# Cumulated decays from a scratch in HBM instead of through TensorE, a pause between a planner's steps, and a copy moved to ScalarE

## The chip, the cores and the metric

One core of a Trainium2 chip runs the whole program. Its engines are TensorE (PE, matrix products and transposes into PSUM), VectorE (DVE), ScalarE (ACT), GpSimd (POOL) and SyncE (SP, which here only issues transfers). Each works its own queue in order and waits for others by semaphores. The metric is the device time of one execution in microseconds (us), as the median of several runs. The profile is one further execution, taken by the hardware profiler.

## The reference

Two layers over 256 tokens of width 1024, and a final norm. The first layer is a mixture of a state space part (SSD, 16 heads of 64) and a gated linear attention (GLA, 8 heads); the second is a causal attention of 16 heads of 64, with a gate. The part that the change touches is the SSD's decay and the GLA's inner product:

```python
def ssd_chunked_scan(xs, dt, a, bm, cm, d_skip):
    ...
    a_cs = jnp.cumsum(dt_c * a, axis=2)
    a_t = jnp.moveaxis(a_cs, 2, -1)
    seg = a_t[..., :, None] - a_t[..., None, :]
    causal = jnp.tril(jnp.ones((Q, Q), dtype=bool))
    decay_ij = jnp.exp(jnp.where(causal, seg, -jnp.inf))
    cb = jnp.einsum('bcign,bcjgn->bcgij', c_c, b_c)
    y_diag = jnp.einsum('bcgeij,bcjgep->bcigep', cb[:, :, :, None] * decay_ij, xdt)
    ...

def ssd_gla_layer(x, ...):
    h = rms_norm(x, norm_w)
    u = h @ w_in
    ...
    y_a = ssd_chunked_scan(xs, dt, a, bm, cm, d)
    y_a = rms_norm(y_a * jax.nn.silu(z_a), ssd_norm_w)
    ...
    o_b = gla_chunked(q_b, k_b, v_b, log_decay)
    o_b = rms_norm(o_b, gla_norm_w) * jax.nn.silu(g_b)
    out = jnp.concatenate([y_a, o_b], axis=-1) @ w_out
    return x + out
```

The kernel must give `rms_norm(x, final_norm)` of both layers' result.

## The kernel before

**Products and weights.** Every large product runs in three parts: weights and activations are cut into a high and a low part (`h_`, `l_`), and high by high, high by low and low by high are summed in PSUM (`mm3`). Weights arrive in pieces of 512 KB or less through SP's queue (`fetch`) into four raw buffers; ScalarE copies the high part (L77) and VectorE subtracts for the low one (L78) into one of seven buffers (`NW`). `need` cuts pieces up to three ahead of the one in use (`AHEAD` = 4). Stages follow one another on TensorE: `pa` and `pb` (input projections of layer 1; `pa` with 416 columns, `pb` with 256), `pc` (output projection, columns from GLA `c1`, from SSD `c0`), `pv` (values of layer 2, two halves `n` of 512 columns, in each two tiles `tt` of 128 tokens, 8 blocks `kb` of three products), `pp` (queries, keys, gates of layer 2) and `pf` (output projection).

**Planner.** All small work beside these products is written as generators (`co_...`) that yield a delay. A clock (`clock["now"]`) advances by an estimated time with each product (`spend`); after each block of three products `due()` runs every generator whose time has come. So the code is written in one fixed order at build time: on TensorE, VectorE and ScalarE the order of instructions follows from it. The delays stand in the table `DL`.

**The mixer** (some 40 to 165 us). `co_first` computes the time steps `dt`, their cumulated decay `acp` (16 heads by 256 tokens), its copy `acT`, a high-low cut of it `ahl`, and by transposes the form with tokens on partitions, `acs`. `co_pair` handles two blocks of two heads: a transpose of `xs` (`xtp`) gives `xdt` (VectorE, L509); for each head a product of a column of ones (`sel`) with `ahl` (`ab`, a small PSUM tile) brings that head's decays to all 128 partitions; ScalarE forms relu(acs - ab) into `e` (L516, L518) and its exponential (L520), VectorE multiplies by the scores `cbT` (L521). After a delay the group `yp` multiplies `e` by `xdt`, and VectorE adds the skip into `y` (L533). `co_gla_pair` handles two heads: scores `gs`; ScalarE copies them to `sT` (L604), POOL masks them (L605), VectorE adds one crossing block (L607); then the values' products `go`, the norm of each head (ScalarE squares, VectorE, POOL's power L625, VectorE), the gated result `ob` (L629), and its transposes `obt` (L163), cut into `obhi` and `oblo`.

**Small PSUM tiles.** `pm` gives one of four small PSUM tiles. A request waits until the last reader of the tile's previous holder is done.

**Between the layers.** `co_turn` transposes a part of `x1` (`htp`, four blocks of 128 columns): for each block ScalarE writes the high part (L741), VectorE the low part (L742), into the activations that `pv` reads (`h`). `co_norm` and its `rb1p` bring the norm's factors to all partitions.

Of the kernel before, what the change touches and what calls it, by code (L numbers as in the profile page):

```python
# [37 lines left out]
C_DTB, C_AL = 79, 95  # L38
C_N = 111

M_ID, M_TRI, M_MASK, M_SEL = 0, 128, 384, 768
M_N = 784


@with_exitstack
def trunk(ctx, tc, xw_d, x_d, cst_d, mat_d, gw2_d, fn_d, wa_d, wb_d, wc_d, wv_d, wp_d, wf_d, out_d):
# [79 lines left out]

    clock = {"now": 0.0, "seq": 0}
    waiting = []  # L130

    def spend(ns):
# [75 lines left out]
    tri = [mat[:, M_TRI + P * i:M_TRI + P * i + P] for i in range(2)]  # L208
    mask = mat[:, M_MASK:M_MASK + 3 * P]
    ones = cpool.tile([P, 1], F32, name="ones")  # L210
    mhalf = cpool.tile([P, 2], F32, name="mhalf")
    V.memset(ones, 1.0)
    V.memset(mhalf, -0.5)
    scanm = big.tile([P, 16, 64], F32, name="scanm", tag="s3")
# [149 lines left out]
    acT = cpool.tile([16, T], F32, name="acT")
    ahl = cpool.tile([P, T], F32R, name="ahl")
    sel = cpool.tile([P, 16], F32R, name="sel")
    G.memset(ahl.bitcast(F32), 0.0)


    gl3 = cpool.tile([P, T], F32R, name="gl3")  # L370
# [7 lines left out]
    def co_first(ps):  # L378
# [38 lines left out]
        for tt in range(2):  # L417
            mm(acp[0:16, tt * P:tt * P + P], dta[:, tt, :], tri[tt])
        V.tensor_copy(acT, acp[0:16, 0:T])
        S.activation(ahl[0:16, :], acp[0:16, 0:T], AF.Copy)  # L420
        V.tensor_sub(ahl[32:48, :], acT, ahl[0:16, :].bitcast(F32))
        V.tensor_copy(sel, mat[:, M_SEL:M_SEL + 16])
        yield DL["act"]
        act = pm("act")
        for tt in range(2):
# [72 lines left out]
    def co_pair(*blks):  # L498


        rows = [slice(64 * j, 64 * j + 64) for j in range(2)]
        es, xds = [], []
        for i, blk in enumerate(blks):
            yield DL[f"pair{i}"]
            tp = pm(f"xtp{blk}")
            for tt in range(2):
                tr(tp[:, tt * P:tt * P + P], xs[:, blk, tt * P:tt * P + P])
            xdt = tmp.tile([P, 2, 2, 64], F32, name=f"xdt{blk}", tag="t1c", bufs=3)
            V.tensor_tensor(xdt, tp[:, 0:T].rearrange("p (a b c) -> p a b c", a=2, b=2),  # L509
                            dt[:, :, 2 * blk:2 * blk + 2][:, :, :, None].to_broadcast([P, 2, 2, 64]), op=ALU.mult)  # L510
            e = tmp.tile([P, 2, 3, P], F32, name=f"e{blk}", tag="t3", bufs=3)
            for j in range(2):
                h = 2 * blk + j
                ab = pm(f"ab{h}")
                mm(ab[:, 0:T], sel[:, h:h + 1].to_broadcast([P, P]), ahl)
                S.activation(e[:, j, 0:2, :].rearrange("p a b -> p (a b)"), ab[:, 0:T], AF.Relu, scale=-1.0,  # L516
                             bias=acs[:, 0, h:h + 1])
                S.activation(e[:, j, 2, :], ab[:, P:T], AF.Relu, scale=-1.0, bias=acs[:, 1, h:h + 1])  # L518
            ef = e.rearrange("p a b c -> p (a b c)")
            S.activation(ef, ef, AF.Exp, scale=-1.0)  # L520
            V.tensor_tensor(e, e, cbT[blk // 4].rearrange("p (a b) -> p a b", a=3)[:, None, :, :]  # L521
                            .to_broadcast([P, 2, 3, P]), op=ALU.mult)
            es.append(e)
# [60 lines left out]
    def co_gla_pair(b):  # L584
# [17 lines left out]
        for h, sp_ in zip(heads, sps):  # L602
            sT = tmp.tile([P, 3, P], F32, name=f"sT{h}", tag="t1d")
            S.activation(sT.rearrange("p a b -> p (a b)"), sp_[:, 0:3 * P], AF.Copy)  # L604
            G.affine_select(out=sT[:, 0:3:2, :], in_=sT[:, 0:3:2, :], pattern=[[0, 2], [1, P]],  # L605
                            compare_op=ALU.is_ge, fill=0.0, base=0, channel_multiplier=-1)
            V.tensor_copy(sT[0:64, 0:3:2, 64:P], sp_[0:64, 384:512].rearrange("p (a b) -> p a b", a=2))  # L607
            sTs.append(sT)
        yield DL["gla1"]
        obs = []  # L610
        for h, sT in zip(heads, sTs):
# [6 lines left out]
            ss = sm.tile([P, 2], F32, name=f"oss{h}", tag="oss")  # L618
            for tt in range(2):
                S.activation(sq[:, tt * P:tt * P + P], op[:, tt * P:tt * P + P], AF.Square,  # L620
                             accum_out=ss[:, tt:tt + 1])
            rr = sm.tile([P, 2], F32, name=f"rr{h}", tag="rr")
            V.tensor_tensor(ss, ss, rsv, op=ALU.mult)
            V.tensor_scalar(ss, ss, EPS, None, op0=ALU.add)
            G.tensor_tensor(rr, ss, mhalf, op=ALU.pow)  # L625
            V.tensor_tensor(rr, rr, rsh, op=ALU.mult)
            ob = tmp.tile([P, T], F32, name=f"ob{h}", tag="t1f")
            for tt in range(2):
                V.scalar_tensor_tensor(ob[:, tt * P:tt * P + P], op[:, tt * P:tt * P + P], rr[:, tt:tt + 1],  # L629
                                       gs[:, tt, vc], op0=ALU.mult, op1=ALU.mult)  # L630
            obs.append(ob)
        yield DL["gla2"]
# [116 lines left out]
    def co_norm():  # L749
        s = sm.tile([P, 2], F32, name="sn", tag="sn")  # L750
        V.tensor_tensor(s, ssn[:, :, 0], ssn[:, :, 1], op=ALU.add)
        V.tensor_scalar(s, s, 1.0 / D, EPS, op0=ALU.mult, op1=ALU.add)
        G.tensor_tensor(r1, s, mhalf, op=ALU.pow)
        V.tensor_scalar(rq, r1, -0.125, None, op0=ALU.mult)
        env["r1"] = True
        yield DL["rb1"]
# [185 lines left out]
def _pack(inp):  # L942
# [73 lines left out]
```

## Time and profile before

| | us |
|---|---|
| median of 3 runs | 340.42 |
| lowest, highest | 338.98, 341.65 |
| profiled execution | 340.22 |
| its span | 338.5 |
| TensorE busy in the span | 327.8 (97%) |
| VectorE, ScalarE, GpSimd busy | 259.4, 232.7, 27.1 |

The span is the time from the first to the last instruction of the profiled execution; 1.7 us of the execution lie around it. Busy time of TensorE counts pipelined products by modelled ends, so that a busy engine need not be at its peak rate: how long a product costs is read from the distance of its start to that of the next one, not from its length. In the rows below, an idle time before an instruction stands in brackets with what ended it.

### The profile page before, as it was taken

Reading aid. Unit: us, or ns where it says so; the run is one execution under the profiler, and the core shown is the slowest. Engines: PE = TensorE matmul, PEld = TensorE weight load, DVE = VectorE, ACT = ScalarE, POOL = GpSimd, SP = SyncE. Lnnn points to the kernel's source line nnn. Section 1 sums busy time; section 2 is a strip of 40 time slices with the busy share of each in tenths; the row PEclk is TensorE's granted clock in tenths of the full one; section 3 lists DMA queues with packets and bytes.
Section 4 is the critical chain, followed back from the end, with each engine's and each line's share of the span. In section 5 each row is a group of like instructions: output and inputs, shape, how many; then the busy total and the mean of one; then the engine's idle time right before and its main releaser. Section 6 shows DMA issues by size and latency. Waiting matters only on the chain.

```text
span 338.5 us, 5905 instructions
## 1 busy us (share of the span) xinstructions
PE 327.8 (97%) x2153; PEld 293.9 (87%) x2153; DVE 259.4 (77%) x543; ACT 232.7 (69%) x501; POOL 27.1 (8%) x44
## 2 busy tenths in 40 slices
PE   8999999999997999999999999999999999999992
PEld 8999999999996979999888888888888887888792
DVE  4978978999999587689964775467869699696563
ACT  6858789959868646678352676475696996969420
POOL 2010000000001211344200000000000000000010
PEclk9999999999999999999999999999999999999997
DMA  7985582575427346241685635756408146070003
GB/s 294 406 266 180 166 257 103 178 241 190 135 95 255 124 141 216 80 152 36 221 286 179 192 122 184 248 166 222 173 24 287 65 141 232 1 248 3 0 2 125
DMA packets 16254, 56.15 MB, mean 166 GB/s; under 512 B 1968, under 2 KB 2480, under 8 KB 16096
## 3 DMA queue, kind: packets, MB, share of 16 engines
q1 hardware_dynamic: 15360, 53.37, 46.6%
q10 hardware_dynamic: 864, 2.39, 2.0%
q8 instruction: 17, 0.28, 0.3%
q14 instruction: 13, 0.11, 0.1%
HBM read 54.71 MB, written 1.05 MB: 165 GB/s over the span
## 4 chain that ended last, share of the span: by engine, by line
PE 49%; DVE 20%; ACT 17%; issue 6%; DMA 4%; POOL 2%; POOLq 0%; ACTq 0%; DVEq 0%
PE pc L159 13%; PE pp L159 10%; PE pv L159 6%; PE pa L159 6%; PE pf L159 5%; DVE l_b L78 3%; PE pb L159 3%; DMA r_b<-in_wb 3%; ACT h_p L77 3%; DVE cu L467 2%; DVE l_p L78 2%; ACT pt L810 2%; ACT h_b L77 2%; ACT pt L814 2%; POOL rr L625 1%
## 5 line engine op out<-in xcount | busy, mean ns | idle before, releaser
L159 PE MATMUL pb<-hh,h_b 128*128 128x256 f32 x416 | 76.4, 285 | 0.0
L159 PE MATMUL pp<-h,h_p 128*128 128x512 f32 x192 | 67.3, 402 | 0.0
L159 PEld LDWEIGHTS pb<-hh,h_b 128*128 128x128 f32 x416 | 64.8, 191 | 0.4 <-issue 0.2
L159 PE MATMUL pb<-hh,l_b 128*128 128x256 f32 x208 | 58.8, 283 | 0.0
L159 PE MATMUL pp<-h,l_p 128*128 128x256 f32 x192 | 50.0, 281 | 0.0
L159 PE MATMUL pa<-h_a,hh 128*128 128x416 f32 x160 | 43.1, 359 | 0.0
L159 PEld LDWEIGHTS pp<-h,h_p 128*128 128x128 f32 x192 | 34.5, 188 | 6.7
L159 PEld LDWEIGHTS pb<-hh,l_b 128*128 128x128 f32 x208 | 39.8, 191 | 0.0
L159 PEld LDWEIGHTS pp<-h,l_p 128*128 128x128 f32 x192 | 36.3, 189 | 2.2
L78 DVE TENSOR_TENSOR l_p<-r_p,h_p 128x1024 fp32r<-128x1024 f32 x24 | 29.2, 1223 | 8.8 <-ACT h_p L77 8.1
L78 DVE TENSOR_TENSOR l_b<-r_b,h_b 128x1024 fp32r<-128x1024 f32 x26 | 31.5, 1216 | 2.1 <-ACT h_b L77 2.0
L77 ACT ACTIVATE h_b<-r_b 128x1024 fp32r<-128x1024 f32 x26 | 27.2, 1062 | 5.8 <-DMA r_b<-in_wb 3.0
L159 PEld LDWEIGHTS pa<-h_a,hh 128*128 128x128 f32 x160 | 30.4, 191 | 0.7 <-ACT h_a L77 0.2
L77 ACT ACTIVATE h_p<-r_p 128x1024 fp32r<-128x1024 f32 x24 | 25.2, 1058 | 1.7 <-PE pv L159 1.6
L159 PE MATMUL pa<-l_a,hh 128*128 128x416 f32 x80 | 25.0, 351 | 0.0
L78 DVE TENSOR_TENSOR l_c<-r_c,h_c 128x1024 fp32r<-128x1024 f32 x16 | 19.9, 1253 | 5.6 <-ACT h_c L77 5.6
L77 ACT ACTIVATE h_c<-r_c 128x1024 fp32r<-128x1024 f32 x16 | 16.9, 1055 | 9.6 <-DMA r_c<-in_wc 5.6
L159 PE MATMUL pv<-h_v,h 128*128 128x512 f32 x64 | 20.2, 391 | 0.0
L810 ACT ACTIVATE pt<-pt,nm 128x128 f32<-128x128 f32 (+1 forms) x32 | 14.2, 445 | 3.0 <-DVE nm L808 3.0
L467 DVE SCALAR_TENSOR_TENSOR cu<-pad,cwh,cu 128x256 f32<-128x256 f32 x30 | 14.5, 482 | 2.1 <-ACT cu L465 1.9
L159 PEld LDWEIGHTS pa<-l_a,hh 128*128 128x128 f32 x80 | 15.1, 189 | 0.2
L352 ACT ACTIVATE pp_s<-pp 128x256 f32<-128x256 f32 x24 | 8.7, 376 | 8.8 <-PE pp L159 8.8
(244 smaller groups left out, 711.8 us busy)
## 6 DMA issues: line engine op xcount, KB each, us to landing
r_b<-in_wb SPq DMA_DIRECT2D x26, 512.0 KB, 4.5
r_p<-in_wp SPq DMA_DIRECT2D x24, 512.0 KB, 4.2
r_c<-in_wc SPq DMA_DIRECT2D x16, 512.0 KB, 3.9
r_a<-in_wa SPq DMA_DIRECT2D x12, 416.0 KB, 3.5
r_v<-in_wv SPq DMA_DIRECT2D x8, 512.0 KB, 4.5
r_f<-in_wf SPq DMA_DIRECT2D x8, 512.0 KB, 4.5
xw<-in_xw SPq DMA_DIRECT2D x6, 546.0 KB, 6.5
x<-in_x ACTq DMA_DIRECT2D x1, 1024.0 KB, 7.2
```

Of the source, the lines that this page charges most:

```text
L77: S.activation(hi, raw, AF.Copy)
L78: V.tensor_sub(lo, raw, hi.bitcast(F32))
L159: TE.matmul(out, lhsT, rhs, start=start, stop=stop)
L352: S.activation(t_, ps[:, T:2 * T], AF.Copy)
L467: V.scalar_tensor_tensor(u, pd[:, 1 + i:1 + i + T], w(i), u, op0=ALU.mult, op1=ALU.add)
L625: G.tensor_tensor(rr, ss, mhalf, op=ALU.pow)
L810: S.activation(pt[:, cs], pt[:, cs], AF.Exp, scale=-1.0, bias=nm[:, tt:tt + 1], accum_out=sme[:, tt:tt + 1])
L814: S.activation(pt[:, cs], pt[:, cs], AF.Copy, scale=sme[:, tt:tt + 1])
```

## The change

Three things are changed.

1. `acT` is written to a scratch `acd` in HBM by two POOL transfers (its second half twice, so that a row has the 384 values of a head in the order of `e`). `co_pair` has POOL load two rows of it onto all 128 partitions, straight into the tile `e`, ahead of its first step; ScalarE's Relu then works in place. `ab`, `ahl`, `sel` and their steps are gone; `e` has four buffers instead of three; `acT` and `gl3` share memory with `ks` and `qs`.
2. `due()` runs no further generator for 1500 ns (`GAP`) of the planner's clock after a step that put work on TensorE. This applies wherever `due()` is called.
3. The crossing block is copied by ScalarE ahead of POOL's mask. The norm's steps of two heads are done as one, so that both `ob` follow one POOL power.

```diff
+GAP = 1500
...
+    dram = ctx.enter_context(tc.tile_pool(name="dram", bufs=1, space=bass.MemoryType.DRAM))
...
     def due():
-        while waiting and waiting[0][0] <= clock["now"]:
+
+        while waiting and waiting[0][0] <= clock["now"] >= clock["hold"]:
+            t = clock["now"]
             step()
+            if clock["now"] > t:
+                clock["hold"] = clock["now"] + GAP
...
         V.tensor_copy(acT, acp[0:16, 0:T])
-        S.activation(ahl[0:16, :], acp[0:16, 0:T], AF.Copy)
-        V.tensor_sub(ahl[32:48, :], acT, ahl[0:16, :].bitcast(F32))
-        V.tensor_copy(sel, mat[:, M_SEL:M_SEL + 16])
+        G.dma_start(acd[:, 0:T], acT)
+        G.dma_start(acd[:, T:T + P], acT[:, P:T])
+        env["acT"] = True
...
+        while "acT" not in env:
+            yield 100
+
+        for blk in blks:
+            e = tmp.tile([P, 2, 3, P], F32, name=f"e{blk}", tag="t3", bufs=4)
+            two = acd[2 * blk:2 * blk + 2, :].rearrange("(o h) t -> o (h t)", o=1)
+            G.dma_start(e.rearrange("p a b c -> p (a b c)"), two.to_broadcast([P, 6 * P]))
+            es.append(e)
...
-            e = tmp.tile([P, 2, 3, P], F32, name=f"e{blk}", tag="t3", bufs=3)
+            e = es[i]
             for j in range(2):
                 h = 2 * blk + j
-                ab = pm(f"ab{h}")
-                mm(ab[:, 0:T], sel[:, h:h + 1].to_broadcast([P, P]), ahl)
-                S.activation(e[:, j, 0:2, :].rearrange("p a b -> p (a b)"), ab[:, 0:T], AF.Relu, scale=-1.0,
-                             bias=acs[:, 0, h:h + 1])
-                S.activation(e[:, j, 2, :], ab[:, P:T], AF.Relu, scale=-1.0, bias=acs[:, 1, h:h + 1])
+                e12 = e[:, j, 0:2, :]
+                S.activation(e12, e12, AF.Relu, scale=-1.0, bias=acs[:, 0, h:h + 1])
+                S.activation(e[:, j, 2, :], e[:, j, 2, :], AF.Relu, scale=-1.0, bias=acs[:, 1, h:h + 1])
...
             S.activation(sT.rearrange("p a b -> p (a b)"), sp_[:, 0:3 * P], AF.Copy)
+            S.activation(sT[0:64, 0:3:2, 64:P], sp_[0:64, 384:512].rearrange("p (a b) -> p a b", a=2), AF.Copy)
             G.affine_select(out=sT[:, 0:3:2, :], in_=sT[:, 0:3:2, :], pattern=[[0, 2], [1, P]],
                             compare_op=ALU.is_ge, fill=0.0, base=0, channel_multiplier=-1)
-            V.tensor_copy(sT[0:64, 0:3:2, 64:P], sp_[0:64, 384:512].rearrange("p (a b) -> p a b", a=2))
...
-            V.tensor_tensor(ss, ss, rsv, op=ALU.mult)
-            V.tensor_scalar(ss, ss, EPS, None, op0=ALU.add)
-            G.tensor_tensor(rr, ss, mhalf, op=ALU.pow)
-            V.tensor_tensor(rr, rr, rsh, op=ALU.mult)
+            ops.append(op)
+
+        rr = sm.tile([P, 2, 2], F32, name=f"rr{b}", tag="rr")
+        pair = lambda a: a[:, None, :].to_broadcast([P, 2, 2])
+        V.tensor_tensor(ss, ss, pair(rsv), op=ALU.mult)
+        V.tensor_scalar(ss, ss, EPS, None, op0=ALU.add)
+        G.tensor_tensor(rr, ss, mhalf.rearrange("p (a b) -> p a b", a=2), op=ALU.pow)
+        V.tensor_tensor(rr, rr, pair(rsh), op=ALU.mult)
+        for i, (h, op) in enumerate(zip(heads, ops)):
```

**TensorE at the last pair of SSD blocks** (before, the stretch around 107 us; `gs` are GLA scores, `pa` weight products). Before:

```order
L159 MATMUL gs_1473<-e_1275,e_1276 64x64
L159 MATMUL gs_1474<-e_1275,e_1276 64x64
L163 MATMUL xtp_1493<-mat,xs 128x128 x2
L159 MATMUL ab_1499<-ahl,sel 128x256
L159 MATMUL ab_1503<-ahl,sel 128x256
L159 MATMUL pa_0_1451<-h_a_0_1375,hh 128x416
L159 MATMUL pa_0_1451<-l_a_0_1376,hh 128x416
L159 MATMUL pa_0_1451<-h_a_0_1375,hh 128x416
```

And now:

```order
L165 MATMUL pa_0_1420<-h_a_2_1396,hh 128x416 x2
L165 MATMUL pa_0_1420<-l_a_2_1397,hh 128x416
L165 MATMUL pa_0_1420<-h_a_2_1396,hh 128x416
L169 MATMUL xtp_1512<-mat,xs 128x128 x2
L165 MATMUL pa_1_1421<-h_a_2_1396,hh 128x416
L165 MATMUL pa_1_1421<-l_a_2_1397,hh 128x416
L165 MATMUL pa_1_1421<-h_a_2_1396,hh 128x416 x2
L165 MATMUL pa_1_1421<-l_a_2_1397,hh 128x416
```

The two `ab` behind the transpose are gone, and the transpose no longer stands next to the scores: weight products are on both sides.

**TensorE at `pv`** (the values of layer 2; `htp` transposes the last quarter of `x1`). Before, in the first tile of 128 tokens:

```order
L159 MATMUL pv_2521<-h_v_2_2453,h_2318 128x512 x2
L159 MATMUL pv_2521<-l_v_2_2454,h_2318 128x512
L159 MATMUL pv_2521<-h_v_2_2453,h_2318 128x512
L159 MATMUL pv_2521<-h_v_3_2524,h_2318 128x512
L159 MATMUL pv_2521<-l_v_3_2525,h_2318 128x512
L159 MATMUL pv_2521<-h_v_3_2524,h_2318 128x512
L163 MATMUL htp_2572<-mat,x_1683 128x128 x4
L163 MATMUL rb1p<-mat,r_2319 128x128 x2
```

And now, in the second tile, `pv_2531`, whose products start right behind `rb1p`:

```order
L169 MATMUL rb1p<-mat,r_2270 128x128 x2
L165 MATMUL pv_2531<-h_v_0_2380,h_2269 128x512
L165 MATMUL pv_2531<-l_v_0_2381,h_2269 128x512
L165 MATMUL pv_2531<-h_v_0_2380,h_2269 128x512 x2
L165 MATMUL pv_2531<-l_v_0_2381,h_2269 128x512
L165 MATMUL pv_2531<-h_v_0_2380,h_2269 128x512
L165 MATMUL pv_2531<-h_v_1_2392,h_2269 128x512
L165 MATMUL pv_2531<-l_v_1_2393,h_2269 128x512
L165 MATMUL pv_2531<-h_v_1_2392,h_2269 128x512
L169 MATMUL htp_2541<-mat,x_1599 128x128 x4
L165 MATMUL pv_2531<-h_v_1_2392,h_2269 128x512
L165 MATMUL pv_2531<-l_v_1_2393,h_2269 128x512
```

The last `htp` has moved behind `rb1p`, from the 21st product of the first tile to the 9th of the second. Three products behind it come those of `h_v_2` and `h_v_3`, which read the blocks that it brings.

**VectorE at the same place** (`h` is the low part from `htp`, `l_v` and `l_p` are weights' low parts). Before:

```order
L742 SCALAR_TENSOR_TENSOR h_2318<-htp_2572,cst,h_2318 128x128 x3
L78 TENSOR_TENSOR l_v_3_2623<-r_v_3_2620,h_v_3_2622 128x1024
L742 SCALAR_TENSOR_TENSOR h_2318<-htp_2572,cst,h_2318 128x128
L78 TENSOR_TENSOR l_p_2635<-r_p_2632,h_p_2634 128x1024
L78 TENSOR_TENSOR l_p_2647<-r_p_2644,h_p_2646 128x1024
```

And now:

```order
L757 SCALAR_TENSOR_TENSOR h_2269<-htp_2449,cst,h_2269 128x128
L80 TENSOR_TENSOR l_v_3_2574<-r_v_3_2571,h_v_3_2573 128x1024
L757 SCALAR_TENSOR_TENSOR h_2269<-htp_2541,cst,h_2269 128x128
L80 TENSOR_TENSOR l_p_2586<-r_p_2583,h_p_2585 128x1024
L757 SCALAR_TENSOR_TENSOR h_2269<-htp_2541,cst,h_2269 128x128 x2
L80 TENSOR_TENSOR l_p_2598<-r_p_2595,h_p_2597 128x1024
L757 SCALAR_TENSOR_TENSOR h_2269<-htp_2541,cst,h_2269 128x128
```

Before, one weight subtraction stood between the four blocks of the last `htp`; now two stand between them and one just ahead. ScalarE's queue has the weights' high copies at the same places.

## Rows read from the trace of the kernel before

**Rows 1.** Page, busy us (share) x instructions of each engine.
```profile
PE 327.8 (97%) x2153; PEld 293.9 (87%) x2153; DVE 259.4 (77%) x543; ACT 232.7 (69%) x501; POOL 27.1 (8%) x44
```
**Rows 2.** Stretch: us, busy PE, PEld, DVE, ACT, POOL, PEclk, DMA share, GB/s.
```profile
100.00:115.00 15.00, 13.07 (x110) 11.16 (x109) 11.85 (x19) 10.65 (x25) 1.91 (x3) 1.00 0.64 210
```
**Rows 3.** TensorE's timeline: start, length, line, operation, shapes, count [idle before, releaser].
```profile
107.28 0.44 PE L163 MATMUL xtp<-mat,xs 128*128 128x128 f32 x2
108.62 0.35 PE L159 MATMUL ab<-ahl,sel 128*128 128x256 f32 x1 [0.91 <-DVE y L533]
110.00 0.38 PE L159 MATMUL ab<-ahl,sel 128*128 128x256 f32 x1 [1.02 <-DVE xdt L509]
110.22 0.35 PE L159 MATMUL pa<-h_a,hh 128*128 128x416 f32 x1
```
**Rows 4.** VectorE's timeline at the same place.
```profile
109.53 0.42 DVE L509 TENSOR_TENSOR xdt<-xtp,dt 128x256 f32<-128x256 f32 x1
```
**Rows 5.** TensorE's timeline at a GLA transpose.
```profile
124.53 0.41 PE L163 MATMUL obt<-mat,ob 128*128 128x128 f32 x2 [0.78 <-DVE y L533]
```
**Rows 6.** TensorE's timeline at two `ab` without a wait.
```profile
60.86 0.48 PE L159 MATMUL ab<-ahl,sel 128*128 128x256 f32 x2
61.18 0.35 PE L159 MATMUL pa<-h_a,hh 128*128 128x416 f32 x1
61.37 0.35 PE L159 MATMUL pa<-l_a,hh 128*128 128x416 f32 x1
```
**Rows 7.** DMA issues: queue, count, KB each, us from issue to landing.
```profile
fnb<-in_fn ACTq DMA_DIRECT2D x1, 512.0 KB, 4.1
gw<-in_gw SPq DMA_DIRECT2D x3, 32.0 KB, 7.4
```
**Rows 8.** VectorE's timeline at the copy of the decays.
```profile
41.43 0.40 DVE L419 COPY acT<-acp 16x256 f32<-16x256 f32 x1
```
**Rows 9.** ScalarE's timeline at the copies of the SSD scores.
```profile
47.12 0.88 ACT L491 ACTIVATE cbT<-cb 128x384 f32<-128x384 f32 x2
```
**Rows 10.** TensorE's timeline in the GLA part.
```profile
113.27 1.60 PE L159 MATMUL go<-v,sT 128*128 128x128 f32 x12
116.98 1.50 PE L159 MATMUL go<-v,sT 128*128 128x128 f32 x12
120.69 1.52 PE L159 MATMUL yp<-e,xdt 128*64 128x256 f32 x16
...
127.34 0.40 PE L159 MATMUL pb<-hh,h_b 128*128 128x256 f32 x2
127.58 0.29 PE L159 MATMUL pb<-hh,l_b 128*128 128x256 f32 x1
```
**Rows 11.** VectorE's timeline, `ob` of the two `go` groups of rows 10.
```profile
118.76 0.61 DVE L629 SCALAR_TENSOR_TENSOR ob<-go,rr,gs 128x128 f32<-128x128 f32 x2
124.30 1.29 DVE L629 SCALAR_TENSOR_TENSOR ob<-go,rr,gs 128x128 f32<-128x128 f32 x4
```
**Rows 12.** TensorE's timeline at the last `htp`.
```profile
206.42 0.60 PE L163 MATMUL htp<-mat,x 128*128 128x128 f32 x4
206.86 0.38 PE L163 MATMUL rb1p<-mat,r 128*128 128x128 f32 x2
...
207.31 0.39 PE L159 MATMUL pv<-l_v,h 128*128 128x512 f32 x1
207.54 0.39 PE L159 MATMUL pv<-h_v,h 128*128 128x512 f32 x1
```
**Rows 13.** VectorE's timeline behind it, low parts `h` of four blocks.
```profile
207.46 0.35 DVE L742 SCALAR_TENSOR_TENSOR h<-htp,cst,h 128x128 fp32r<-128x128 f32 x1 [0.92 <-ACT h L741]
208.25 0.35 DVE L742 SCALAR_TENSOR_TENSOR h<-htp,cst,h 128x128 fp32r<-128x128 f32 x1 [0.44 <-ACT h L741]
...
210.45 1.23 DVE L78 TENSOR_TENSOR l_v<-r_v,h_v 128x1024 fp32r<-128x1024 f32 x1 [1.01 <-ACT h_v L77]
211.59 0.34 DVE L742 SCALAR_TENSOR_TENSOR h<-htp,cst,h 128x128 fp32r<-128x128 f32 x1
```

More of the change, by code (lines that the diff above doesn't have):

```diff
@@ L39 @@
 C_N = 111
-M_ID, M_TRI, M_MASK, M_SEL = 0, 128, 384, 768
-M_N = 784
+M_ID, M_TRI, M_MASK = 0, 128, 384
+M_N = 768
 @with_exitstack
@@ L124, in trunk @@
         plan_tm(f"f{n}", wf_d[n])
-    clock = {"now": 0.0, "seq": 0}
+    clock = {"now": 0.0, "seq": 0, "hold": 0.0}
     waiting = []
@@ L210, in trunk @@
     ones = cpool.tile([P, 1], F32, name="ones")
-    mhalf = cpool.tile([P, 2], F32, name="mhalf")
+    mhalf = cpool.tile([P, 4], F32, name="mhalf")
     V.memset(ones, 1.0)
@@ L363, in trunk @@
     acs = st("acs")
[L364 to L370, printed above, removed]
+    acT = big.tile([16, T], F32, name="acT", tag="ks")
+    acd = dram.tile([16, 3 * P], F32, name="acd")
+    gl3 = big.tile([P, T], F32R, name="gl3", tag="qs")
     gw3 = big.tile([P, 512], F32R, name="gw3", tag="s2")
@@ L522, in co_pair @@
                             .to_broadcast([P, 2, 3, P]), op=ALU.mult)
-            es.append(e)
             xds.append(xdt)
@@ L604, in co_gla_pair @@
             S.activation(sT.rearrange("p a b -> p (a b)"), sp_[:, 0:3 * P], AF.Copy)
+            S.activation(sT[0:64, 0:3:2, 64:P], sp_[0:64, 384:512].rearrange("p (a b) -> p a b", a=2), AF.Copy)
             G.affine_select(out=sT[:, 0:3:2, :], in_=sT[:, 0:3:2, :], pattern=[[0, 2], [1, P]],
                             compare_op=ALU.is_ge, fill=0.0, base=0, channel_multiplier=-1)
-            V.tensor_copy(sT[0:64, 0:3:2, 64:P], sp_[0:64, 384:512].rearrange("p (a b) -> p a b", a=2))
             sTs.append(sT)
         yield DL["gla1"]
-        obs = []
-        for h, sT in zip(heads, sTs):
+        obs, ops = [], []
+        ss = sm.tile([P, 2, 2], F32, name=f"oss{b}", tag="oss")
+        for i, (h, sT) in enumerate(zip(heads, sTs)):
             op = pm(f"go{h}")
@@ L617, in co_gla_pair @@
             sq = tmp.tile([P, T], F32, name=f"osq{h}", tag="t1e")
-            ss = sm.tile([P, 2], F32, name=f"oss{h}", tag="oss")
             for tt in range(2):
                 S.activation(sq[:, tt * P:tt * P + P], op[:, tt * P:tt * P + P], AF.Square,
-                             accum_out=ss[:, tt:tt + 1])
-            rr = sm.tile([P, 2], F32, name=f"rr{h}", tag="rr")
-            V.tensor_tensor(ss, ss, rsv, op=ALU.mult)
-            V.tensor_scalar(ss, ss, EPS, None, op0=ALU.add)
-            G.tensor_tensor(rr, ss, mhalf, op=ALU.pow)
-            V.tensor_tensor(rr, rr, rsh, op=ALU.mult)
+                             accum_out=ss[:, i, tt:tt + 1])
+            ops.append(op)
[6 more added lines that the diff above has]
+        for i, (h, op) in enumerate(zip(heads, ops)):
+            vc = slice(P * h, P * h + P)
             ob = tmp.tile([P, T], F32, name=f"ob{h}", tag="t1f")
             for tt in range(2):
-                V.scalar_tensor_tensor(ob[:, tt * P:tt * P + P], op[:, tt * P:tt * P + P], rr[:, tt:tt + 1],
+                V.scalar_tensor_tensor(ob[:, tt * P:tt * P + P], op[:, tt * P:tt * P + P], rr[:, i, tt:tt + 1],
                                        gs[:, tt, vc], op0=ALU.mult, op1=ALU.mult)
@@ L752, in co_norm @@
         V.tensor_scalar(s, s, 1.0 / D, EPS, op0=ALU.mult, op1=ALU.add)
-        G.tensor_tensor(r1, s, mhalf, op=ALU.pow)
+        G.tensor_tensor(r1, s, mhalf[:, 0:2], op=ALU.pow)
         V.tensor_scalar(rq, r1, -0.125, None, op0=ALU.mult)
@@ L974, in _pack @@
     mat[:, M_MASK + 2 * P:M_MASK + 3 * P] = low
-    mat[0:16, M_SEL:M_SEL + 16] = mat[32:48, M_SEL:M_SEL + 16] = np.eye(16, dtype=f)
     wo = a["odd_w_in"][0]
```

## The prediction

> **What bounds the kernel now.** I read the busy shares first: TensorE is at work for 327.8 us of 338.5, 97% [rows 1]. A change can therefore only take TensorE work away, close one of its few idle places, or open a new one; time saved on VectorE (77%) or ScalarE (69%) counts only where TensorE stands and waits for it. The stretches show where that is: between 100 and 115 us TensorE is busy for 13.07 of 15 us [rows 2]. TensorE's timeline there names the places. At 107.28 two transposes of `xs` (`xtp`) are followed by the two `ab` products of a pair, and each waits: 0.91 us for VectorE's `y` (L533) and 1.02 us for its `xdt` (L509); the weight product `pa` that stands behind them starts at 110.22 [rows 3]. VectorE ends that `xdt` at 109.53 + 0.42 = 109.95, just ahead of the second `ab` at 110.00 [rows 4]. `ab` computes nothing that needs `y` or `xdt`: it waits for a free one of the four small PSUM tiles, which they read. A second place is at 124.53, where a transposed GLA output (`obt`) waits 0.78 us for `y` [rows 5], for the same reason.
>
> The profiled execution took 340.22 us, of which the span is 338.5 and 1.7 lie around it; the median of the runs shown is 340.42, 0.2 above. I sum against the span and add 1.7.
>
> **Part 1, the decays through HBM.** Removed from TensorE: 16 `ab` products. Two of them take from 60.86 to the next product at 61.18, 0.32 us [rows 6]; some of that is the change from one shape to another, which remains behind `xtp`, so I take 0.13 each: 16 x 0.13 = **-2.1 us**.
>
> With them go 16 of the small PSUM tiles, so the wait at 107.28 goes too. In the new order one transpose stands alone among weight products (first pair of lists under the change) and `xdt`'s tile is not asked for at once. The stretch lasted 110.22 - 107.28 = 2.94 us [rows 3]; the work in it, two transposes and two `ab` at the same rate, is some 0.45. That is **-2.5 us**. The wait at 124.53 loses its cause in the same way, **-0.8 us** [rows 5].
>
> ScalarE's 32 Relu steps remain, now with SBUF as input; I count them the same. ScalarE and VectorE lose one small step each before `act` (L420, L421). VectorE idles in that stretch and TensorE does not wait there: zero, and if the cover were gone, well below 1 us.
>
> Added: two small POOL transfers to the scratch and eight loads that spread two rows of it over 128 partitions (393 KB each). No transfer of this kind stands in the trace. The nearest rows are the spread load of the final norm (`fnb`, 512 KB, 4.1 us) as the lower bound of a hop and the slowest issue (`gw`, 7.4 us) as the upper one [rows 7]. `acT` is complete at 41.43 + 0.40 = 41.83 [rows 8], and two hops one after the other bring the first `e` at 50.0 to 56.6. In the new ScalarE order the first Relu stands right behind the two copies `cbT`, which end at 47.12 + 0.88 = 48.0 [rows 9]. ScalarE then stands for 2.0 to 8.6 us, and the weight copies queued behind it stand too (VectorE's subtractions and, last, TensorE wait for those). The planner cuts weights three pieces ahead; a piece of `pa` is 12 products of 0.19 us [rows 6], so the cover is about 7 us. At the bounds that leaves 0 or 1.6 us on TensorE. I take **0**, nearer to the spread load, which has this form. The later loads are issued one or two pairs ahead of use; POOL's next step behind them, a `qs` copy, waits with them in its queue, and its reader, the first GLA scores, comes only around 107 [rows 3].
>
> The Trainium skill (*DMA: Bandwidth & Descriptors*, section "Anatomy of one DMA — SWDGE (gpsimd) path") puts a transfer issued by POOL at 2.0 us plus its bytes over 436,000 a microsecond. As an estimate from that page the two hops are 2.1 and 2.9 us, the first `e` is there at 46.8, and ScalarE never stands. The 512 KB load would be 3.2 us by it and took 4.1 here [rows 7], so the row, not the rule, sets the sum; both give 0.
>
> **Part 2, the crossing block and the merged norm.** VectorE's eight small copies go to ScalarE ahead of POOL's mask. Scores (`gs`) and values (`go`) now stand some 30 products apart, so this chain of about 2 us has cover and costs 0. Merged, however, both heads' `ob` come after one POOL step, and `go`'s two PSUM tiles stay taken until then. Before, the time from a `go` to its `ob` was 119.37 - 113.27 = 6.1 us and 125.59 - 116.98 = 8.6 us [rows 10, 11]. In the new order there are, from `go_1659` to `obt_1746`, which needs its tile: the `go` pair (1.5 us), 15 `pb` products at 0.12, the `yp` group (1.5), 15 more `pb` and one pair of transposes (0.2), 6.8 us [rows 10]. The new wait is thus 0 to 1.8 us; I take **+1.0**, nearer to the second row, since this stretch too has VectorE's `y` ahead of `ob`. For the last pair, from `go_1985` to `obt_2081`, which reads its `ob`, 1.5 + 36 x 0.12 + 0.4 = 6.2 us stand: 0 to 2.4 by the two rows. Little other work is left for VectorE there, so I stay near the first row: **+0.3**.
>
> **Part 3, steps kept apart.** The planner's new pause holds in the whole program, not only in the mixer. It moves the last `htp` (transposes of `x1`, the second half of its columns for the last 128 tokens) from the 21st product of the first `pv` tile to the 9th product of the second (second pair of lists). From there only three products separate it from those that read the blocks it delivers; the block needed last (kb 7, low half) is read by the 15th product behind it. With 0.23 us a product and 0.44 for the transposes that is 3.6 us after the start of `htp` [rows 12]. What ScalarE and VectorE need for its four blocks:
> - Bare, at the cadence of 208.25 - 207.46 = 0.8 us a block: 0.7 us until the first copy, four cadences, 3.9 in all: a wait of 0.3 us.
> - As before with one weight subtraction between: from 206.42 to 211.59 + 0.34 = 211.93, 5.5 us: a wait of 1.9. TensorE did not feel it there, since the reader was far behind [rows 12, 13].
> - In the new orders of ScalarE and VectorE three weight copies and three subtractions of 1.23 us [rows 13] stand between the four blocks (third pair of lists). A walk through both queues, each block's ScalarE step waiting for VectorE's previous one, gives 6.8 to 7.1: a wait of 3.2 to 3.5.
>
> I take **+3.2**, since the order is fixed and these steps are in it.
>
> **Sum.** -2.1 - 2.5 - 0.8 + 1.0 + 0.3 + 3.2 = -0.9 us. Span 338.5 - 0.9 = 337.6, time **339.3 us**.
>
> **Rivals.**
> - *A, the late htp is cheap.* If the weight copies do not delay the blocks (they wait for buffers that `pv` frees, and may find them free long before), only the bare wait of 0.3 remains: -2.1 - 2.5 - 0.8 + 1.0 + 0.3 + 0.3 = -3.8, **336.4 us**; with no `ob` wait either, -5.1, 335.1. For it: the copy at 210.45 was itself late, 1.01 us behind ScalarE [rows 13]. Against it: the queues are worked in order.
> - *B, VectorE's arrears stay.* The waits at 107 and 124 come from VectorE being late with `y` and `xdt`. If its arrears turn up at other small tiles, 3.3 us are not gained: **342.6 us**. For it: VectorE loses hardly any work. Against it: half of the requests for small tiles in this part are gone.
> - *C, the loads come late (slower).* If the scratch hop takes 7.4 us, the spread load 7.4 too, and the four loads that stand together in POOL's queue, with the weights of SP beside them, cost the first one 4.1 us more [rows 7], the first `e` is there at 41.8 + 7.4 + 7.4 + 4.1 = 60.7. ScalarE stands 12.7 us, 5.7 more than the cover: **345.0 us**. It decides from a landing after 55 us, and the verdict turns at about 59.5. For it: TensorE has no slack in that stretch and POOL's queue is in order. Against it: two hops at the spread load's 4.1 us land at 50. The Trainium skill speaks for this rival (*SBUF — State Buffer*, the warning on "DVE blocks DMA"): while VectorE runs a plain fp32 copy within SBUF, POOL cannot write the descriptors of its transfers. Nearly all of VectorE's work there is arithmetic on two inputs, and no run shown here has a POOL transfer to test it.
>
> **Chances and range.** The forecast (all six terms as taken) 0.42; A 0.30; B 0.13; C 0.15. A measurement of this kernel can tell about 1%, so faster means below 337.0 and slower above 343.8. A is the faster side, 0.30; forecast and B are within 1%, 0.55; C is slower, 0.15. The range reaches down into A, short of its extreme, to 335.6 and up past B to 343.0, and leaves out C and a little of A, some 2 in 10. The likeliest case's own range runs from 336.7 (1.9 us at `htp`, no `ob` wait) to 342.5 (3.5, 1.8 and 2.4).
>
> **What would show it.** After the change the trace should have no idle place at an `xtp`, busy time of TensorE lower by about 2 us, a wait of some 3 us on VectorE's `h` in the second `pv` tile, and a wait of at most 1.8 us at an `obt` in front of VectorE's `ob`. If TensorE runs through the `pv` stretch without a pause, A holds. If the first Relu of `e` starts after 57 us and weight products pause between 55 and 75, C holds. Waits for `y` or `xdt` at other tiles show B. The prediction falls as a whole if TensorE waits at a place not named here.

## The result, and the profile after

The changed kernel takes 342.73 us (median of 19 runs, 340.80 to 345.44) against 340.02 for the kernel before on the same chips: a ratio of 1.0071, 95% interval 1.0050 to 1.0091. It is slower by 0.7%. That is inside "no change" by the 1% that I had set, and inside the range, but on the other side of zero than the forecast of 339.3, and clear of noise. It also lies beside rival B's 342.6, by chance: B's sign, waits for `y` or `xdt` at other tiles, is absent from the list of waits below. So the question is where the gain in the mixer went.

The profiled execution took 344.32 us, 1.6 more than the median, so a loss read from its trace is larger than the ratio says. Its span is 342.6 us. These are parts 1 and 2 of its page (busy us and share of each engine; then tenths of 40 slices of 8.6 us, PEclk being the granted clock):

```profile
PE 329.7 (96%) x2137; PEld 293.3 (86%) x2137; DVE 254.1 (74%) x521; ACT 234.1 (68%) x508; POOL 32.1 (9%) x49
PE   8999999979999999999999998899999999999992
PEclk9999999989999999999999999999999999999997
```

TensorE has 16 products fewer and is busy 1.9 us longer than in [rows 1]. That alone says that part of its work ran slowly, and the ninth slice names the place. The list of TensorE's waits (who waited for whom: us in total, times, longest) names the others:

```profile
PE pb L165 <- DVE gs L293: 1.8, 1, 1.8
PE pv L165 <- DVE h L757: 1.4, 3, 0.5
PE warmp L183 <- DVE mhalf L219: 1.3, 1, 1.3
PE pv L165 <- ACT h L756: 0.5, 1, 0.5
PE go L165 <- POOL sT L616: 0.5, 1, 0.5
...
```

The waits for `y` and `xdt` of [rows 3, 5] are gone and no `obt` waits. Instead there is one of 1.8 us at a `pb`, and the ones at `pv` that the forecast had named.

I set the same TensorE products of both traces side by side, numbering the products of `pa`, `pb`, `pc`, `pv` and taking the difference of their start times. The first `pc` starts at 156.19 us before and 156.23 after: **the mixer gained next to nothing** (0.5 us of its gain only makes up for a later start, since the first `pb` stands at +0.48). The first `pv` product stands at +0.12. Between the 37th and the 49th `pv` product the changed kernel loses 3.6 us, and it keeps that to the end: 342.6 against 338.5.

**What happens before the first `pc`.** The chain that ended last (start, length, what), where it leads through the scratch:

```profile
43.03 0.69 POOL acd L425
...
43.73 3.14 DMA acd<-acT
...
47.43 6.95 DMA e<-acd
...
54.40 0.51 ACT e L528
```

The write into the scratch takes 3.1 us, the first spread load 7.0. ScalarE's timeline shows that it stands 4.21 us ahead of the Relu for it; VectorE's shows what is then late; and TensorE's what waits:

```profile
54.40 0.51 ACT L528 ACTIVATE e<-e,acs 128x256 f32<-128x256 f32 x1 [4.21 <-DMA e<-acd]
...
57.95 0.42 DVE L476 SCALAR_TENSOR_TENSOR xs<-cth,cu 128x256 f32<-128x256 f32 x1 [6.14 <-ACT cth L474]
...
63.76 2.29 DVE L451 TENSOR_TENSOR_SCAN gcs<-scanm,gmn 128x1024 f32<-128x1024 f32 x1
67.93 2.36 DVE L80 TENSOR_TENSOR l_b<-r_b,h_b 128x1024 fp32r<-128x1024 f32 x2
70.54 1.08 DVE L293 SCALAR_TENSOR_TENSOR gs<-gth,pa 128x416 f32<-128x416 f32 x2
...
71.17 0.51 PE L165 MATMUL pb<-hh,h_b 128*128 128x256 f32 x2 [1.79 <-DVE gs L293]
...
73.09 0.63 PE L165 MATMUL pb<-hh,h_b 128*128 128x256 f32 x2
73.51 0.41 PE L165 MATMUL pb<-hh,l_b 128*128 128x256 f32 x1
73.73 0.63 PE L165 MATMUL pb<-hh,h_b 128*128 128x256 f32 x2
```

ScalarE's stand makes the decay chain of the GLA (Exp, Ln, then VectorE's scan) late; VectorE then has scan, weight subtractions and `gs` all at once (at L293 this is the GLA's gate, not the scores of the same name); and this `gs` is the reader of a large PSUM tile that TensorE wants for the next `pb`. After the wait three products take 0.64 us (73.09 to 73.73) where [rows 10] have 0.36 (two `h_b` in 0.24, one `l_b` in 0.12). The stretches show why (us, busy PE, PEld, DVE, ACT, POOL, PEclk, DMA share, GB/s):

```profile
69.00:71.20 2.20, 0.41 (x5) 0.21 (x3) 2.20 (x5) 2.20 (x4) 0.00 (x0) 1.00 0.46 123
72.20:75.40 3.20, 3.20 (x17) 3.20 (x16) 3.20 (x6) 2.74 (x6) 0.00 (x0) 0.50 0.62 178
```

TensorE stood for most of the 2.2 us up to 71.2, and from 72.2 to 75.4 its granted clock was 0.50, 1.2 instead of 2.4 GHz. The 15 products from 72.23 to 75.43 take 3.2 us where 1.8 would do at 0.36 for three: another 1.4 us, and part of the busy time that TensorE has more.

**What happens at `pv`.** TensorE's and VectorE's timelines behind the last `htp`, which starts at 209.58:

```profile
209.58 0.60 PE L169 MATMUL htp<-mat,x 128*128 128x128 f32 x4
...
211.72 1.05 PE L165 MATMUL pv<-h_v,h 128*128 128x512 f32 x2 [0.35 <-DVE h L757]
213.54 0.90 PE L165 MATMUL pv<-h_v,h 128*128 128x512 f32 x2 [0.53 <-DVE h L757]
215.44 0.50 PE L165 MATMUL pv<-h_v,h 128*128 128x512 f32 x1 [0.54 <-ACT h L756]
216.71 0.73 PE L165 MATMUL pv<-h_v,h 128*128 128x512 f32 x2 [0.53 <-DVE h L757]
...
210.18 1.23 DVE L80 TENSOR_TENSOR l_v<-r_v,h_v 128x1024 fp32r<-128x1024 f32 x1 [3.29 <-ACT h_v L79]
211.32 0.34 DVE L757 SCALAR_TENSOR_TENSOR h<-htp,cst,h 128x128 fp32r<-128x128 f32 x1
212.00 1.23 DVE L80 TENSOR_TENSOR l_p<-r_p,h_p 128x1024 fp32r<-128x1024 f32 x1 [0.34 <-ACT h_p L79]
213.14 0.34 DVE L757 SCALAR_TENSOR_TENSOR h<-htp,cst,h 128x128 fp32r<-128x128 f32 x1
213.92 0.35 DVE L757 SCALAR_TENSOR_TENSOR h<-htp,cst,h 128x128 fp32r<-128x128 f32 x1 [0.44 <-ACT h L756]
215.17 1.23 DVE L80 TENSOR_TENSOR l_p<-r_p,h_p 128x1024 fp32r<-128x1024 f32 x1 [0.90 <-ACT h_p L79]
216.31 0.34 DVE L757 SCALAR_TENSOR_TENSOR h<-htp,cst,h 128x128 fp32r<-128x128 f32 x1
```

Each of the four blocks is waited for, and three weight subtractions of 1.23 us stand just ahead of them and among them. From the start of `htp` to the product that reads the last low part it takes 216.71 - 209.58 = 7.1 us where 3.6 would do. The idle times in the list of waits add up to only 1.9 us; the 3.6 us are read from the distances of the starts.

### The profile page after: what moved, and what is told of

It is laid out like the page before. It is cut to its first block, busy times and chain, and to the rows that moved or that the text cites. A ratio compares the mean times of both kernels' runs of the same rounds, so it can differ in the third digit from the quotient of the medians.

```text
span 342.6 us, 5883 instructions
## 1 busy us (share of the span) xinstructions
PE 329.7 (96%) x2137; PEld 293.3 (86%) x2137; DVE 254.1 (74%) x521; ACT 234.1 (68%) x508; POOL 32.1 (9%) x49
## 4 chain that ended last, share of the span: by engine, by line
PE 56%; ACT 17%; DVE 12%; DMA 9%; issue 3%; POOL 1%; POOLq 0%; ACTq 0%; SPq 0%; DVEq 0%
PE pc L165 13%; PE pb L165 10%; PE pp L165 10%; PE pa L165 6%; PE pv L165 6%; PE pf L165 5%; DMA e<-acd 4%; ACT h_p L79 3%; DVE l_p L80 3%; ACT pt L825 2%; ACT h_b L79 2%; DVE l_b L80 2%; ACT pt L829 2%; DMA r_b<-in_wb 1%; DMA r_a<-in_wa 1%
## 5 line engine op out<-in xcount | busy, mean ns | idle before, releaser
L165 PE MATMUL pb<-hh,h_b 128*128 128x256 f32 x416 | 79.1, 291 | 1.8 <-DVE gs L293 1.8
L165 PEld LDWEIGHTS pb<-hh,h_b 128*128 128x128 f32 x416 | 65.8, 195 | 3.1 <-DVE gs L293 2.0
L165 PE MATMUL pb<-hh,l_b 128*128 128x256 f32 x208 | 59.5, 286 | 0.0
L165 PEld LDWEIGHTS pb<-hh,l_b 128*128 128x128 f32 x208 | 40.5, 195 | 0.0
L165 PE MATMUL pv<-h_v,h 128*128 128x512 f32 x64 | 21.6, 405 | 2.0 <-DVE h L757 1.4
L165 PEld LDWEIGHTS pv<-h_v,h 128*128 128x128 f32 x64 | 11.9, 188 | 6.8 <-DVE h L757 3.0
```

The costliest lines, as they stand in the source:

```text
L165: TE.matmul(out, lhsT, rhs, start=start, stop=stop)
```

## The experiments

Two theories came out of this. **H**: the pause, which holds beyond the mixer, moves the last `htp` too close to its readers, 3.6 us. **L**: the first load from the scratch lands late, ScalarE stands in its queue, TensorE waits and then runs at half clock, 1.8 + 1.4 = 3.2 us or more. Rivals: VectorE's load, the place of the Relu steps in the queue, or a gain at one place that is given back at the next. Ratios are to the kernel before, run on the same chip (340.89 us in the first four runs, 340.34 in the others).

**The pause taken away in the whole program.**

```diff
-GAP = 1500
+GAP = 0
```

> The changed kernel with the planner's pause set to 0; the loads from the scratch and the merged norm stay. Theory H (the late htp costs what TensorE stands at pv): htp is back ahead of rb1p, the waits of 2.0 us at pv and the slow products beside them go, 3.6 us less than the changed kernel's 342.7, so 339.1, ratio to before 0.997. If in the mixer the pause is what keeps TensorE from waiting at 107 us, 1 to 2.5 us of waits at small tiles come back there and it is 340 to 341.6. Rival (the pause is not what costs; the loss at pv is VectorE's arrears): a wait of some 2 us at pv stays and the time is 342 to 343. Theory L (the first loads land late) has the wait of 1.8 us near 69 us in all cases.

Measured: 341.89 us, 1.0016 (0.9985 to 1.0047). No wait at `pv`, as H has it; in the profile TensorE passes from the first `pc` to the first `pp` without changing its distance to the kernel before (-0.98 and -1.02 us). The wait of L is still there: ScalarE stands 2.35 us for the load, VectorE 4.65 behind it, and 2.1 us of TensorE are lost at a `pb` that here waits for the low part of its weights. The waits of [rows 3] do not come back, so the pause was not needed to remove them. The ratio is that of some 340.6 us beside the 340.02 of the result, in the middle of the 340 to 341.6 expected for the case that they come back; some 1.5 us are missing all the same against the next run. Where is not shown: the profiled execution here is the fastest of its twelve, that of the next run the slowest.

**The pause only in the mixer.**

```diff
     drain()
+    clock["gap"] = clock["hold"] = 0.0
     obhi, oblo = env["ob"]
```

(`due()` reads `clock["gap"]` in place of `GAP`.)

> The changed kernel, its pause set to 0 once the mixer is over; the mixer is untouched. Theory H: no wait at pv, 3.6 us less, 339.1 us, ratio to before 0.997; TensorE's timeline up to the first pc as in the changed kernel, with the wait of 1.8 us near 69 us. Rival (what is saved at pv is lost again at the first pp, whose weights were cut under the wait): 341 to 342.7.

Measured: 340.34 us, 0.9973 (0.9951 to 0.9994). The changed kernel would take 343.3 beside this kernel before (340.89 x 1.0071), so 3.0 us less by the median, 3.3 by the two ratios; H predicted 3.6. No wait at `pv`, and nothing is lost at `pp`. The wait of L is there and longer in this profile, 3.0 us, with the half clock behind it (TensorE's timeline, then stretches, columns as above):

```profile
72.02 0.80 PE L165 MATMUL pb<-hh,h_b 128*128 128x256 f32 x2 [3.02 <-DVE gs L293]
72.00:73.00 1.00, 0.98 (x4) 0.98 (x5) 1.00 (x2) 0.89 (x1) 0.00 (x0) 0.50 0.82 291
73.00:77.00 4.00, 4.00 (x21) 4.00 (x20) 4.00 (x7) 3.50 (x8) 0.00 (x0) 0.50 0.65 199
```

**The first Relu steps later.** The first two blocks take `acs` from a second transposition of `acT`, placed ahead of the first `xtp`, so ScalarE's queue has the GLA's steps and weight copies first.

```diff
+            first = env.setdefault("pair", blks) == blks
+            if first and i == 0:
+                again = pm("again")
+                for tt in range(2):
+                    TE.transpose(again[:, 16 * tt:16 * tt + 16], acT[:, tt * P:tt * P + P], ident[0:16, 0:16])
+                V.tensor_copy(acl, again[:, 0:32].rearrange("p (a b) -> p a b", a=2))
+            ac = acl if first else acs
...
-                S.activation(e12, e12, AF.Relu, scale=-1.0, bias=acs[:, 0, h:h + 1])
+                S.activation(e12, e12, AF.Relu, scale=-1.0, bias=ac[:, 0, h:h + 1])
```

> The changed kernel with one edit: the Relu steps of the first two blocks read the decays from a second transposition that TensorE makes just ahead of the first xtp, near 59 us, so ScalarE's queue has other steps where it stood 4.2 us for the first load. Theory L (ScalarE's stand of 4.2 us is behind TensorE's wait of 1.8 us near 69 us and behind the half clock that follows it): no wait of TensorE there, the granted clock stays at full, 1.8 to 3.5 us less than 342.7: 339.2 to 340.9, ratio 0.998 to 1.003. Rival (VectorE has too much to do there whatever the load does): the wait of 1 to 2 us is still there, 342 to 343.

Measured: 339.47 us, 0.9970 (0.9956 to 0.9985): 3.8 us less than the 343.3, or 3.4 by the two ratios. That is at and a little past the upper end of what L says (3.5, and 0.998). No wait near 69 us; between 72.2 and 75.4 TensorE has 29 products instead of 17, at full clock. The first `pc` starts 5.1 us ahead of the kernel before (the first `pb` 0.5). The waits at `pv` remain. The rival is out: VectorE is busy 15.00 of 15 us from 70 to 85 here, as in the changed kernel, and TensorE does not stand (stretches, columns as above; the first is of the changed kernel, the others are of this run):

```profile
70.00:85.00 15.00, 13.83 (x105) 13.24 (x106) 15.00 (x25) 13.08 (x26) 1.07 (x2) 0.89 0.76 217
...
70.00:85.00 15.00, 15.00 (x130) 14.41 (x129) 15.00 (x26) 15.00 (x32) 1.07 (x2) 1.00 0.70 197
...
72.20:75.40 3.20, 3.20 (x29) 3.20 (x29) 3.20 (x6) 3.20 (x8) 0.00 (x0) 1.00 0.79 178
```

**Both edits together.**

> Both edits at once: pause only in the mixer, and the first Relu steps later. If the two costs are independent, as theories H and L together say: 342.7 - 3.6 - 1.8 to 3.5 = 335.6 to 337.3 us, ratio 0.987 to 0.992. If the gain in the mixer is eaten by something else: 338.5 to 339.5, as with the first edit alone.

Measured: **335.6 us, 0.9851 (0.9829 to 0.9872)**, 7.7 us below the 343.3 (7.5 by the ratios) and just below the 0.987 expected. The two edits alone gave 3.0 and 3.8 (3.3 and 3.4 by the ratios), so the costs add up, and together they give a little more; why is not shown. This version beats both kernels by 1.5% and more. Of the list of TensorE's waits there is left:

```profile
PE warmp L183 <- DVE mhalf L219: 1.3, 1, 1.3
PE as L165 <- DVE qkl L887: 0.3, 1, 0.3
PE pa L165 <- ACT h_a L79: 0.2, 1, 0.2
```

**The loads left out.** This tells the late landing from the place of the Relu steps. What is left out is the decays' transfer: the exponents of the SSD part are formed from zeros.

```diff
-            G.dma_start(e.rearrange("p a b c -> p (a b c)"), two.to_broadcast([P, 6 * P]))
+            G.memset(e, 0.0)
```

> The changed kernel with the eight loads from the scratch left out: POOL sets the tiles e to zero instead, so the decays in the SSD part are wrong, and ScalarE's queue keeps the Relu steps in the place that they have in the changed kernel. Theory L says that only the landing of the first load is late, not the place of the steps: ScalarE does not stand near 50 us, TensorE does not wait near 69 us, the clock stays full, and the time is that of the run with later Relu steps, 3 to 4 us below the changed kernel, ratio to before 0.996 to 0.999. Rival (the place of the Relu steps in ScalarE's queue delays the weights by itself): the wait near 69 us stays, at 1 us or more, and the ratio is 1.003 to 1.007. In both cases the waits of 2 us at pv are there.

Measured: 339.56 us, 0.9981 (0.9964 to 0.9998), as the later Relu steps gave. The Relu steps stand where the changed kernel has them and nobody stands (ScalarE's timeline):

```profile
49.84 0.60 ACT L470 ACTIVATE cu<-pad,cwh 128x256 f32<-128x256 f32 x1
50.33 0.51 ACT L528 ACTIVATE e<-e,acs 128x256 f32<-128x256 f32 x1
```

So the place of the Relu steps alone costs nothing. In the run with later Relu steps the first load landed as late (53.8 us), with all loads in place, and cost nothing either: it takes both, a load that lands late and an instruction that waits for it ahead of other work. L holds. The waits at `pv` are there as expected.

**The pause alone, in the kernel before.** `GAP` and the hold in `due()` as in the change, all else as before.

> The kernel before with nothing but the planner's pause of 1500 ns. Theory H: the last htp moves behind rb1p as in the changed kernel, and TensorE stands about 2 us at pv and loses 3.7 us there. In the mixer the steps stand apart, so the waits of 0.9, 1.0 and 0.8 us at small tiles should shrink: 0 to 2.7 us back. Together ratio 1.003 to 1.011. Rival (the pause removes nothing in the mixer as long as ab asks for 16 small tiles): 1.010 to 1.015.

Measured: 342.62 us, 1.0076 (1.0055 to 1.0098). The waits of 0.9, 1.0 and 0.8 us are gone even with all 16 `ab`, so the pause alone would have removed them, and that rival is out; a new one of 1.4 us stands at the last `obt`. The first `pc` is 1.2 us early, and between the 37th and 49th `pv` product the same 3.6 us are lost as in the changed kernel.

```profile
PE obt L167 <- DVE ob L633: 1.4, 1, 1.4
PE pv L163 <- DVE h L746: 1.4, 3, 0.5
...
PE pv L163 <- ACT h L745: 0.5, 1, 0.5
```

**Later Relu steps, no pause at all.** (`GAP = 0` in that kernel.)

> The kernel with later Relu steps and no pause at all. With the pause only in the mixer it took 335.6 us (0.985 of before). If the pause is worth something in the mixer once the loads no longer delay ScalarE, waits at small tiles come back and it is 337 to 338.5 (0.989 to 0.993). If the loads alone emptied the small tiles, it is the same, 335.3 to 336.3 (0.984 to 0.987).

Measured: 337.13 us, 0.9906 (0.9877 to 0.9936). Against 0.9851 with the pause in the mixer, the pause is worth some 0.5% there (1.9 us by the ratios); the two intervals just fail to touch. Its list of waits has 0.5 us at a `yp` and 0.2 at a `gs`. Its profiled execution had a span of 334.1 us, next to 334.0 with the pause, so where the difference lies is not shown.

**The crossing block and the norm as before.** The best kernel with that part of the change undone: VectorE copies the crossing block behind POOL's mask, and each head has its own norm steps.

```diff
-            S.activation(sT[0:64, 0:3:2, 64:P], sp_[0:64, 384:512].rearrange("p (a b) -> p a b", a=2), AF.Copy)
             G.affine_select(out=sT[:, 0:3:2, :], in_=sT[:, 0:3:2, :], pattern=[[0, 2], [1, P]],
                             compare_op=ALU.is_ge, fill=0.0, base=0, channel_multiplier=-1)
+            V.tensor_copy(sT[0:64, 0:3:2, 64:P], sp_[0:64, 384:512].rearrange("p (a b) -> p a b", a=2))
...
-        V.tensor_tensor(ss, ss, pair(rsv), op=ALU.mult)
+            V.tensor_tensor(ss, ss, rsv, op=ALU.mult)
```

> The best kernel so far (later Relu steps, pause only in the mixer) with the crossing block and the GLA norm as before the change. My forecast had 1.3 us of new waits at obt from the merged norm; no trace since shows them. If the merging costs nothing and saves little: 335 to 336.3 us, 0.984 to 0.987. If the merged steps relieve VectorE and POOL where TensorE waits for them: 336.5 to 338, 0.988 to 0.992. If it costs hidden time: 334 to 335, 0.980 to 0.983.

Measured: 338.07 us, 0.9936 (0.9912 to 0.9960), 0.85% or 2.9 us slower than with it, a little past the 0.992 expected for the case that the merged steps relieve VectorE and POOL. Its waits show where:

```profile
PE obt L169 <- DVE ob L647: 1.4, 1, 1.4
...
PE go L165 <- DVE sT L625: 1.0, 1, 1.0
```

2.4 us are the two that this part removes: the last `obt` in front of `ob`, and a `go` in front of VectorE's crossing copy.

## Why the prediction was wrong, step by step

| step | forecast, us | measured, us |
|---|---|---|
| 16 `ab` products less | -2.1 | -1.8 (8 x 0.23) |
| waits at 107 us | -2.5 | gone, also with the pause alone and with no pause |
| wait at 124 us | -0.8 | gone |
| first loads from the scratch | 0 | +3.4 (late Relu) or +3.1 (no loads) by ratios |
| merged norm, crossing block | +1.3 | 0: no wait at `obt` (undone in the best version: +2.9) |
| last `htp` | +3.2 | +3.6 |

**Right: the removal.** The products [rows 6]: two `ab` and the `pa` behind them take 0.51 us from 60.86 to 61.37. In the changed kernel the `pa` behind the transposes takes 0.28, 0.23 less; I count this eight times:

```profile
59.19 0.44 PE L165 MATMUL pa<-h_a,hh 128*128 128x416 f32 x1
59.47 0.35 PE L165 MATMUL pa<-l_a,hh 128*128 128x416 f32 x1
```

What the waits at 107 and 124 us are worth was not measured one by one. With both costs out (both edits together), the first `pc` starts 4.9 us ahead of the kernel before and the first `pb` 0.3, so the mixer gains some 4.5 us where these three terms make 5.4.

**Right: the late `htp`.** The walk through ScalarE's and VectorE's queues gave 6.8 to 7.1 us; the trace has 7.1. With the pause out of that stretch the 3.6 us are gone, with the pause alone they appear.

**Wrong, and decisive: the loads.** The sentence that fails is "I take **0**, nearer to the spread load, which has this form". Two parts of it were wrong, and the second is what failed. First, the price: the write took 3.1 us, less than either bound (4.4 from 43.03 to the issue of the load at 47.43), and the first spread load 7.0, close to the upper bound of 7.4 and not the lower of 4.1. This alone would not have moved the term: a landing at 54.4 is inside the 50.0 to 56.6 that I had, and ScalarE's stand (4.2 us measured, 6.4 from my 48.0) is inside the cover of 7, so the working gives 0 for it too. The nearest row by its form was not the nearest by its surroundings: `fnb` of [rows 7] was issued at 78.0 us, in a stretch (70 to 85) with a mean transfer share of 0.66, and the first `e` comes where nearly all 16 are taken. In the changed kernel these stretches stand around it (DMA share is the last column but one):

```profile
48.00:50.00 2.00, 2.00 (x18) 2.00 (x19) 1.43 (x3) 2.00 (x4) 1.67 (x4) 1.00 0.99 341
52.00:54.00 2.00, 2.00 (x19) 2.00 (x18) 0.00 (x0) 0.00 (x0) 0.00 (x0) 1.00 0.96 346
```

A rule that bears on it is in the Trainium skill, *DMA: Bandwidth & Descriptors*, section "Issuing engines are not separate DMA queues": transfers of all engines end up on the same 16 and interleave. These rows agree: with SP's weights and POOL's loads under way, 341 and 346 GB/s at a share of 0.96 to 0.99. By the fit of the same page of the Trainium skill that I had weighed (2.0 us plus bytes over 436,000), the load would be 2.9 us as an estimate; here it took 7.0. In the run with later Relu steps the same load took 6.6 us at the first place (share near 1.0) and 3.4 at 91.8 us, where the share was 0.4. So the price goes with what else is under way, the two loads issued right behind the first one among it; no run changes that alone.

Second, the cover. The first `e` landed at 54.4 us, before the 55 from which I let rival C decide, and the wait came all the same. I had counted how far ahead weights are cut, and the weights were in time: the low part for the waiting `pb` was done at 69.15 us, just before TensorE stopped at 69.4 (without a pause it is the weights that come late). What ran out was VectorE: it had no work from 51.8 to 57.95, then everything of that time on top of its own, and the reader of a large PSUM tile came too late. A stand in an in-order queue must be followed into everything behind it, here the GLA's gate, not only into the chain that one has in mind. And the wait cost more than itself: behind 1.8 us of standing came 3.4 us of half clock, 1.4 us more, for which the sum had no term.

So rival C named the beginning of the mechanism, with the wrong price and threshold: of its two signs the pause of weight products between 55 and 75 came, the first Relu after 57 did not (54.40). Its warning from the Trainium skill (*SBUF — State Buffer*), that VectorE's plain copies keep POOL from writing descriptors, is not what happened: POOL issued three loads in 1.64 us, and they were late on the transfer engines. VectorE ran arithmetic on two inputs and no plain copy meanwhile, so the warning itself was not tested.

```profile
47.43 1.64 POOL L514 DMA_DIRECT2D e<-acd  x3 [3.20 <-DMA acd<-acT]
```

**Wrong: the merged norm.** I expected waits at `obt_1746` and at the last `obt` and measured none at either. I had taken the old chain from `go` to `ob` [rows 10, 11] for the new one. But in the old one VectorE and POOL take turns twice for two heads, and the merging makes that once. For the last pair these are the starts of `go` and `ob` in the changed kernel, then in the run with the norm as before:

```profile
149.19 1.50 PE L165 MATMUL go<-v,sT 128*128 128x128 f32 x12
154.86 1.12 DVE L644 SCALAR_TENSOR_TENSOR ob<-go,rr,gs 128x128 f32<-128x128 f32 x4
...
145.94 1.50 PE L165 MATMUL go<-v,sT 128*128 128x128 f32 x12
152.98 1.11 DVE L647 SCALAR_TENSOR_TENSOR ob<-go,rr,gs 128x128 f32<-128x128 f32 x4
```

The chain is 5.7 us merged and 7.0 not; against the 6.2 that I had counted as standing in between, the first leaves no wait, and the difference is about the 1.4 that the second waits. At the earlier place TensorE does the four transposes of `obt` at 132.96 without a wait, ahead of the `ob` at 133.74, so they did not need the tile that I held them to need. Undone, this part costs 2.9 us.

The sum with the measured terms, and the waits at 107 and 124 as forecast, -1.8 - 2.5 - 0.8 + 3.4 + 3.6, is +1.9; the ratio says 2.4. The merged norm is left out of this sum: the waits of 1.4 and 1.0 us that it removes were not in the kernel before, and the first of them comes with the pause alone.

## What to carry to other kernels

A product that only spreads data can be replaced by a load, but the load's price must be read where it will run: at a transfer share near 1.0 the same load took 6.6 to 7.0 us, and 3.4 at a share of 0.4, and its waiting instruction must not stand in an in-order queue ahead of work that others need. A rule added to a planner for one stage should end with that stage: here 1500 ns of pause gave some 1.5 to 1.9 us in the mixer and cost 3.6 us behind it. And when two good parts and two side effects are measured as one change, the result says little: the parts are worth 1.5% once the two side effects are out.

## What was not expected of the hardware

TensorE's clock fell to half behind a stand of 1.8 us in a stretch that is otherwise full, for 3.4 us, and again for 3.4 behind one of 2.1 us in the run without a pause. With the stand of 3.0 us it was at half for 6.8 us, from 71.1 to 77.9, the first of them while TensorE still stood. It did not fall behind the waits at `pv` (0.35 to 0.54 us each in the list, granted clock 1.00), nor behind the 1.4 us at the last `obt` in the two runs that have it.

The half clock does not come alike in every execution. The 19 runs of the changed kernel have granted clocks from 0.986 to 0.996, as means over the run, and 3.4 us at half take 0.005 off such a mean. The eight runs at 0.993 or more took 340.8 to 342.3 us, the other eleven 342.7 to 345.4; the profiled one, at 0.989, is among the latter. Two kernels with later Relu steps, which have no such stand, lie within 1.0 us (ten runs) and 0.2 us (four runs). But the stand is not all there is to it: two others with later Relu steps spread over 3.2 us (no pause, six runs, clocks 0.989 to 0.998) and 1.9 us (norm as before, six runs), and the kernel before, whose trace shows no fall, over 4.0 us (27 runs, clocks 0.985 to 0.998).
